# A SwiGLU feed-forward on one core: weight-block differences on GpSimd instead of VectorE

## The chip, the cores and the metric

The kernel runs on one core of one Trainium2 chip. The metric is device time of one execution in microseconds. The engines are named as in the profile: PE (TensorE matmul) and PEld (its weight load), DVE (VectorE), ACT (ScalarE), POOL (GpSimd) and SP (SyncE, here the queue that issues nearly all DMAs).

## What is computed

One encoder layer on 1024 tokens of width 1024: a token mixer, then a SwiGLU channel mixer, all in float32. The change lies in the channel mixer, with a hidden width of 2816:

```python
h = rms_norm(x) * (1 + sc2) + sh2
x = x + g2 * ((jax.nn.silu(h @ ffn_w_gate[l]) * (h @ ffn_w_up[l])) @ ffn_w_down[l])
```

## The kernel before

The hidden width is cut into NF = 22 column tiles of 128. For each tile the products with the gate and the up weights are formed as one 2x2 block product by Strassen-Winograd: seven block products instead of eight, with differences of weight blocks (T1 to T4) and of activation blocks (S1 to S4) as operands. Each float32 operand is split into a high and a low float32r part (`split`: a copy on ACT at L233, a subtraction on DVE at L239), and each block product is three passes of four 128x128 by 128x512 matmuls, so 12 matmuls (`product`, L1606).

The function `ffn` has three stages.

- **Stage one** (loop at L1655): for each tile the two products that need the plain gate weights. Their sums p1 and s1 go to DRAM (tensor `psd`).
- **Stage two** (loop at L1717): for each tile f the other five products, in the order X with T2 (PSUM tile X), Y with T1 (PSUM tile Y), X with T3, Y with block B22, X with T4. Names in the profile: `T12h`/`T12l` hold T1 and T2, `T3h`/`T3l` hold T3 and B22, `t4s` holds T4. DVE adds the partial sums between them: L1739 after the first X product, L1741 after the first Y product, L1745, L1747, L1749, then L1754 and L1756 for the second half. PE waits for L1739 before it adds T3 to X, for L1741 before it adds B22 to Y and for L1745 before it adds T4 to X. Differences of rows of the down weights and of activations, tiles x and y (both named `sx`), are formed on the way for stage three (L1743, L1751, L1759 in the first 11 tiles, L1762, L1763, L1765 in the last 11) and stored (`td`, `s3d`, `sd`, `s4d`).
- **Stage three** (L1834 on): the down projection out of the stored operands.

The weight blocks of a tile are made by `weights(f)` at L1667: loads of `wg` and `wu` (L1617, 512 KB each), two differences into `t12`, one into `wu` in place, one into `t4`, and the three splits. It is called at high priority, ahead of its tile. `wg`, `wu`, `t12` and `t4` have two buffers each, and so have the split tiles. So the load of `wu` for tile f+4 waits until the split T3l of tile f+2 has read its buffer, and the load of `wg` for tile f+4 waits until the last difference (L1678) of tile f+2 has read its. The tiles x and y share three buffers.

A scheduler writes one fixed order for each engine from the code and its priorities. Each engine, and SP's queue of DMAs too, then works strictly in that order: an instruction or a DMA that waits holds all that stand behind it.

Of the kernel before, what the change touches and what calls it, by code (L numbers as in the profile page):

```python
# [12 lines left out]
ALU = mybir.AluOpType  # L13
# [1568 lines left out]
def ffn(K, sp, S, at):  # L1582
# [4 lines left out]
    nc, d = K.nc, K.d  # L1587
    V = nc.vector
# [20 lines left out]
    def pair(t, slots, name):  # L1609

        hi, lo = (S.tile([P, NK, P], F32R, s, name + n) for s, n in zip(slots, "hl"))
        K.split(hi, lo, t)
        return [(hi[:, c], lo[:, c]) for c in (slice(0, 4), slice(4, 8))]

    def load(src, f, slot):
        t = S.tile([P, NK, P], F32, slot, src)
        nc.sync.dma_start(t, d[src][f])  # L1617
        return t
# [48 lines left out]
    def weights(f):  # L1667
        wg, wu = load("wg", f, (22, 8)), load("wu", f, (24, 9))
        t12 = S.tile([P, NK, P], F32, (26, 10), "t12")
        t4 = S.tile([P, 4, P], F32, (19, 16), "t4")  # L1670
        B11, B21, B12, B22 = wg[:, 0:4], wg[:, 4:8], wu[:, 0:4], wu[:, 4:8]
        w = {}
        V.tensor_tensor(t12[:, 0:4], B12, B11, op=ALU.subtract)
        V.tensor_tensor(t12[:, 4:8], B22, t12[:, 0:4], op=ALU.subtract)
        w["T1"], w["T2"] = pair(t12, ((28, 11), (29, 14)), "T12")
        V.tensor_tensor(B12, B22, B12, op=ALU.subtract)
        w["T3"], w["22"] = pair(wu, ((20, 12), (23, 15)), "T3")
        V.tensor_tensor(t4, B21, t12[:, 4:8], op=ALU.subtract)  # L1678
        hl = S.tile([P, 2, 4, P], F32R, (25, 13), "t4s")
        K.split(hl[:, 0], hl[:, 1], t4)  # L1680
        w["T4"] = hl[:, 0], hl[:, 1]
        return w
# [32 lines left out]
    with K.first():  # L1715
        ws = [weights(0)]
    for f in range(NF):  # L1717
        ps1 = S.tile([P, 2, H], F32, (27, 0, 1, 2), "psr")
        nc.sync.dma_start(ps1, K.psd[f])
        if f + 1 < NF:  # L1720
            with K.first():
                ws.append(weights(f + 1))
        else:
            more(3)
# [153 lines left out]
```

## Time and profile before

| | us |
|---|---|
| three runs | 1514.78, 1514.87, 1522.44 |
| median | 1514.87 |
| profiled execution, its own time | 1520.79 |
| span of the profiled execution | 1518.9 |
| PE busy | 1389.5 |
| DVE busy | 1118.4 |
| ACT busy | 542.5 |
| POOL busy | 90.9 |

The span is the time from the first to the last instruction of the profiled execution; its own time is 1.9 us longer. Busy time is summed over instructions of an engine. In the trace stage one runs from about 815 us, stage two from about 980 to 1294 us, and stage three to the end.

### The profile page before, as it was taken

To read this page: it belongs to the slowest core of one execution; us is meant where nothing else is said; L and a number is where in the kernel's file an instruction comes from. 1 tells how busy PE (TensorE), PEld (TensorE's weight loads), DVE (VectorE), ACT (ScalarE), POOL (GpSimd) and SP (SyncE) were. 2 spreads that over 40 slices of the span, in tenths; PEclk is the share of its full clock that TensorE was granted. 3 is DMA by queue.
4 is the path that set the end of the run, shared out by engine and by line. 5 is a ranking of instruction groups with operands and counts; after the bars stand their busy time and mean duration, and the time that the engine had idled before them with its cause. 6 is when DMAs were issued, how large, how long until landed. Compare 5 with 4: busy or idle time off the path is not lost.

```text
span 1518.9 us, 19510 instructions
## 1 busy us (share of the span) xinstructions
PE 1389.5 (91%) x6717; PEld 1115.8 (73%) x6717; DVE 1118.4 (74%) x2123; ACT 542.5 (36%) x973; POOL 90.9 (6%) x143
## 2 busy tenths in 40 slices
PE   2589989998998998999998999999999999999995
PEld 0366768776787767877776777887778878888884
DVE  7999977887756684687865458378777887557588
ACT  2522221232142342333545766322222222434352
POOL 2110000000101231320000000000000000000000
PEclk9789999999998999989999999999999999999998
DMA  6634366577662324476435448677776776977762
GB/s 248 196 101 146 121 198 217 181 240 222 205 195 93 114 84 154 118 250 223 151 102 180 146 164 285 230 258 249 254 246 218 234 266 239 331 236 244 238 221 110
DMA packets 160598, 300.31 MB, mean 198 GB/s; under 512 B 27871, under 2 KB 72831, under 8 KB 160500
## 3 DMA queue, kind: packets, MB, share of 16 engines
q1 hardware_dynamic: 137204, 271.77, 54.6%
q10 hardware_dynamic: 22688, 25.99, 4.8%
q0 software_dynamic: 608, 1.31, 0.3%
q8 instruction: 53, 0.87, 0.2%
q14 instruction: 45, 0.37, 0.1%
HBM read 221.12 MB, written 77.89 MB: 197 GB/s over the span
## 4 chain that ended last, share of the span: by engine, by line
PE 59%; DVE 14%; DMA 9%; issue 3%; ACT 1%; POOL 1%; SPq 0%; POOLq 0%; DVEq 0%; ACTq 0%
PE Z L1606 8%; PE X L1606 6%; PE dx L1844 6%; PE Y L1606 5%; PE gps L495 5%; PE gps L507 4%; PE dz L1844 4%; PE dy L1844 4%; PE gps L1556 3%; DMA mxw<-modw 3%; DMA wu<-wu 2%; PE nS L1429 2%; PE ops L1556 1%; PE nS L1407 1%; DVE wlo L239 1%
## 5 line engine op out<-in xcount | busy, mean ns | idle before, releaser
L495 PE MATMUL gps<-hhi,whi 128*128 128x512 f32 x320 | 130.3, 407 | 3.8 <-ACT nt L531 3.8
L495 PE MATMUL gps<-hlo,whi 128*128 128x512 f32 x320 | 128.9, 403 | 0.0
L495 PE MATMUL gps<-hhi,wlo 128*128 128x512 f32 x320 | 128.4, 401 | 0.0
L239 DVE TENSOR_TENSOR dl<-dr,dh 128x1024 fp32r<-128x1024 f32 x77 | 93.5, 1221 | 37.4 <-ACT dh L233 25.2
L233 ACT CAST dh<-dr 128x1024 fp32r<-128x1024 f32 x77 | 80.4, 1052 | 104.6 <-PE dz L1844 30.0
L1606 PE MATMUL Z<-hp,wgh 128*128 128x512 f32 x352 | 95.8, 402 | 1.0 <-ACT ps L1661 0.9
L507 PE MATMUL gps<-whi,hhi 128*128 128x256 f32 (+1 forms) x256 | 76.8, 300 | 1.5 <-ACT z L531 1.5
L1606 PEld LDWEIGHTS Z<-hp,wgh 128*128 128x128 f32 x352 | 63.6, 188 | 19.2 <-ACT ps L1661 4.7
L507 PE MATMUL gps<-whi,hlo 128*128 128x256 f32 (+1 forms) x256 | 76.8, 300 | 0.0
L507 PE MATMUL gps<-wlo,hhi 128*128 128x256 f32 (+1 forms) x256 | 76.3, 298 | 0.0
L495 PEld LDWEIGHTS gps<-hhi,whi 128*128 128x128 f32 x320 | 60.5, 189 | 19.3 <-ACT nt L531 5.0
L233 ACT CAST T3h<-wu 128x1024 fp32r<-128x1024 f32 x22 | 23.1, 1052 | 132.0 <-PE Y L1606 121.1
L495 PEld LDWEIGHTS gps<-hhi,wlo 128*128 128x128 f32 x320 | 60.2, 188 | 13.7 <-issue 1.6
L495 PEld LDWEIGHTS gps<-hlo,whi 128*128 128x128 f32 x320 | 60.4, 189 | 12.2 <-issue 0.8
L1500 DVE SCALAR_TENSOR_TENSOR mxacc<-mxw,cond,mxacc 128x512 f32<-128x512 f32 x56 | 41.9, 748 | 32.4 <-DMA mxw<-modw 32.2
L1606 PE MATMUL X<-A,t4s 128*128 128x512 f32 x264 | 63.6, 390 | 0.1
L1606 PEld LDWEIGHTS X<-A,t4s 128*128 128x128 f32 x264 | 49.5, 188 | 10.8 <-DVE uv L1745 0.5
L507 PEld LDWEIGHTS gps<-whi,hhi 128*128 128x128 f32 x256 | 49.9, 195 | 3.1 <-ACT z L531 1.9
L1606 PE MATMUL Y<-AS,T3h 128*128 128x512 f32 x176 | 45.5, 400 | 7.3 <-DVE uv L1741 7.3
L1844 PE MATMUL dx<-dh,dl 128*128 128x512 f32 x132 | 51.4, 389 | 0.0
L1844 PE MATMUL dx<-dh 128*128 128x512 f32 x132 | 51.4, 389 | 0.0
L1844 PE MATMUL dx<-dl,dh 128*128 128x512 f32 x132 | 51.4, 389 | 0.0
(521 smaller groups left out, 3511.2 us busy)
## 6 DMA issues: line engine op xcount, KB each, us to landing
wg<-wg SPq DMA_DIRECT2D x44, 512.0 KB
mxw<-modw SPq DMA_DIRECT2D x64, 256.0 KB
raw<-w_in SPq DMA_DIRECT2D x28, 512.0 KB
dr<-wd SPq DMA_DIRECT2D x55, 256.0 KB
psd<-ps SPq DMA_DIRECT2D x22, 512.0 KB
psr<-psd SPq DMA_DIRECT2D x22, 512.0 KB
wu<-wu SPq DMA_DIRECT2D x22, 512.0 KB
ad<-a SPq DMA_DIRECT2D x22, 512.0 KB
```

The source lines that it names most:

```text
L233: nc.scalar.copy(hi, src)
L239: e.tensor_tensor(lo, src, hi.bitcast(F32), op=ALU.subtract)
L495: nc.tensor.matmul(ps, lhsT=w[:, k, c], rhs=x[k][:, t], start=n == 0, stop=n == len(seq) - 1)
L507: nc.tensor.matmul(ps, lhsT=x[k][:, t], rhs=w[:, k, :N], start=n == 0, stop=n == len(seq) - 1)
L1407: nc.tensor.matmul(pb[:, :nk], lhsT=qt[r, i], rhs=ktv[r, r0:r0 + nr, f * 24:f * 24 + 40], start=True, stop=True)
L1429: nc.tensor.matmul(pb[:, 448:512], lhsT=pT[:w * 40, n], rhs=vw[:w * 40, n, c:c + 64], start=n == 0, stop=n == len(chunks) - 1)
L1500: V.scalar_tensor_tensor(acc, in0=mt, scalar=K.cond[:, k:k + 1], in1=acc, op0=ALU.mult, op1=ALU.add)
L1556: K.nc.tensor.matmul(ps, lhsT=l, rhs=r, start=n == 0, stop=n == 5)
L1606: nc.tensor.matmul(ps, lhsT=w[a][:, k], rhs=x[k][b], start=start and n == 0, stop=n == 11, skip_group_check=not start)
L1844: nc.tensor.matmul(acc[i], lhsT=a[:, 0, ts], rhs=b[:, 1], start=first and m == 0, stop=final and m == 2, skip_group_check=n in (2, 3, 5, 6))
```

## The change

The four differences of `weights` go from DVE to POOL. The splits stay where they were. One line is added, so that the lines behind it have a number higher by one in the changed kernel (L1673 becomes L1674, L1678 becomes L1679, L1743 becomes L1744).

```diff
-        V.tensor_tensor(t12[:, 0:4], B12, B11, op=ALU.subtract)
-        V.tensor_tensor(t12[:, 4:8], B22, t12[:, 0:4], op=ALU.subtract)
+        G = nc.gpsimd
+        G.tensor_tensor(t12[:, 0:4], B12, B11, op=ALU.subtract)
+        G.tensor_tensor(t12[:, 4:8], B22, t12[:, 0:4], op=ALU.subtract)
         w["T1"], w["T2"] = pair(t12, ((28, 11), (29, 14)), "T12")
-        V.tensor_tensor(B12, B22, B12, op=ALU.subtract)
+        G.tensor_tensor(B12, B22, B12, op=ALU.subtract)
         w["T3"], w["22"] = pair(wu, ((20, 12), (23, 15)), "T3")
-        V.tensor_tensor(t4, B21, t12[:, 4:8], op=ALU.subtract)
+        G.tensor_tensor(t4, B21, t12[:, 4:8], op=ALU.subtract)
```

The scheduler makes a new order out of it. On DVE, from the end of tile 5 to the start of tile 6, in the first half of stage two (numbers behind a name tell tiles apart: `uv_9384` and `a_9438` are of tile 5, `uv_9489` and x, `sx_9483`, of tile 6), before:

```order
L1747 TENSOR_TENSOR uv_9384<-Y_9383,uv_9384 128x512
L239 TENSOR_TENSOR T3l_9476<-wu_9464,T3h_9475 128x1024
L1749 TENSOR_TENSOR a_9438<-uv_9384,psr_9355 128x512
L1754 TENSOR_TENSOR psr_9355<-X_9382,psr_9355 128x512
L239 TENSOR_TENSOR t4s_9480<-t4_9467,t4s_9480 128x512
L1743 TENSOR_TENSOR sx_9483<-sx_9483 128x512
L1756 TENSOR_TENSOR a_9438<-uv_9384,psr_9355 128x512
L1739 TENSOR_TENSOR uv_9489<-X_9487,psr_9460 128x512
L1673 TENSOR_TENSOR t12_9676<-wu_9674,wg_9672 128x512
```

and in the changed kernel:

```order
L1748 TENSOR_TENSOR uv_9384<-Y_9383,uv_9384 128x512
L239 TENSOR_TENSOR T3l_9476<-wu_9464,T3h_9475 128x1024
L1750 TENSOR_TENSOR a_9438<-uv_9384,psr_9355 128x512
L1744 TENSOR_TENSOR sx_9483<-sx_9483 128x512
L1755 TENSOR_TENSOR psr_9355<-X_9382,psr_9355 128x512
L239 TENSOR_TENSOR t4s_9480<-t4_9467,t4s_9480 128x512
L1752 TENSOR_TENSOR sx_9483<-sx_9484,sx_9483 128x512
L1757 TENSOR_TENSOR a_9438<-uv_9384,psr_9355 128x512
L1740 TENSOR_TENSOR uv_9489<-X_9487,psr_9460 128x512
L1760 TENSOR_TENSOR sx_9379<-a_9438 128x512
L1742 TENSOR_TENSOR uv_9489<-Y_9488,psr_9460 128x512
L239 TENSOR_TENSOR T12l_9576<-t12_9571,T12h_9575 128x1024
```

The differences are gone from DVE, and both steps on x (`sx_9483`, L1744 and L1752) now stand ahead of L1757 of tile 5 and of L1740, the first sum of tile 6.

On SP's queue at the same place, from one load of `wu` (tile 9) to the next (tile 10), before (`td6`, `s3d5` and `ad5` are stores of tiles 6 and 5; of the two loads of `sx`, here of tile 7, the one of 128x1024 is x and the one of 128x512 is y):

```order
L1617 DMA wu_9674<-wu 128x1024
L1757 DMA ad5_135<-a_9438 128x1024
L1719 DMA psr_9775<-psd9_165 128x1024
L1760 DMA s3d5_205<-sx_9379 128x512
L1617 DMA wg_9882<-wg 128x1024
L1752 DMA td6_184<-sx_9483 128x1024
L1728 DMA sx_9588<-wd 128x1024
L1729 DMA sx_9589<-wd 128x512
L1617 DMA wu_9779<-wu 128x1024
```

and in the changed kernel, with two rows of the tile ahead:

```order
L1720 DMA psr_9670<-psd8_164 128x1024
L1729 DMA sx_9483<-wd 128x1024
L1617 DMA wu_9674<-wu 128x1024
L1753 DMA td6_184<-sx_9483 128x1024
L1758 DMA ad5_135<-a_9438 128x1024
L1617 DMA wg_9882<-wg 128x1024
L1761 DMA s3d5_205<-sx_9379 128x512
L1730 DMA sx_9589<-wd 128x512
L1720 DMA psr_9775<-psd9_165 128x1024
L1729 DMA sx_9588<-wd 128x1024
L1617 DMA wu_9779<-wu 128x1024
```

The store `s3d5` and the load of x (`sx_9588`) now stand behind the load of `wg`, and the load of x is the last before the next `wu`.

## Rows read from the trace of the kernel before

**Rows 1.** The page, part 1: busy time, share of the span and instructions of each engine.

```profile
PE 1389.5 (91%) x6717; PEld 1115.8 (73%) x6717; DVE 1118.4 (74%) x2123; ACT 542.5 (36%) x973; POOL 90.9 (6%) x143
```

**Rows 2.** Windows: both halves of stage two; stretch, its length, busy time by engine.

```profile
993.50:1139.70 146.20, 139.35 (x604) 112.42 (x603) 116.44 (x171) 33.57 (x41) 0.00 (x0) 1.00 0.73 248
1139.70:1294.20 154.50, 153.38 (x670) 124.91 (x669) 123.89 (x176) 37.27 (x45) 0.00 (x0) 1.00 0.70 240
```

**Rows 3.** Waits of PE in stage two: us in total, times, longest.

```profile
PE Y L1606 <- DVE uv L1741: 7.3, 9, 1.2
```

**Rows 4.** Timeline of PE: start, us, engine, line, operation, out and in, count.

```profile
1080.57 2.88 PE L1606 MATMUL X<-A,t4s 128*128 128x512 f32 x12
1083.29 1.30 PE L1606 MATMUL X<-AS,T12h 128*128 128x512 f32 x5
```

**Rows 5.** Timeline of SP's queue, one tile of the first half.

```profile
1067.61 1.29 SPq L1617 DMA_DIRECT2D wu<-wu  x1
...
1077.09 0.33 SPq L1617 DMA_DIRECT2D wg<-wg  x1
1078.29 0.32 SPq L1752 DMA_DIRECT2D td<-sx  x1
...
1082.40 0.33 SPq L1729 DMA_DIRECT2D sx<-wd  x1
1082.83 0.38 SPq L1617 DMA_DIRECT2D wu<-wu  x1
```

**Rows 6.** Timeline of DVE, first half of stage two; in brackets the idle time ahead.

```profile
1065.71 0.69 DVE L1747 TENSOR_TENSOR uv<-Y,uv 128x512 f32<-128x512 f32 x1 [1.91 <-PE Y L1606]
1066.32 1.22 DVE L239 TENSOR_TENSOR T3l<-wu,T3h 128x1024 fp32r<-128x1024 f32 x1
...
1072.83 0.69 DVE L1673 TENSOR_TENSOR t<-wu,wg 128x512 f32<-128x512 f32 x1 [1.20 <-DMA wu<-wu]
...
1077.59 0.68 DVE L1751 TENSOR_TENSOR sx<-sx 128x512 f32<-128x512 f32 x1
...
1087.07 0.69 DVE L1673 TENSOR_TENSOR t<-wu,wg 128x512 f32<-128x512 f32 x1 [0.38 <-DMA wu<-wu]
...
1139.69 0.69 DVE L1747 TENSOR_TENSOR uv<-Y,uv 128x512 f32<-128x512 f32 x1 [1.91 <-PE Y L1606]
```

**Rows 7.** Waits of SP's queue in stage two: us in total, times, longest.

```profile
SPq L1617 <- DVE t L1678: 35.4, 17, 4.3
```

**Rows 8.** Groups of POOL: count, then busy us, mean ns, then idle time before.

```profile
L239 POOL TENSOR_TENSOR hlo<-tm,hhi 128x512 fp32r<-128x512 f32 x8 | 11.9, 1492 | 47.3 <-DVE hhi L235 47.3
...
L429 POOL TENSOR_TENSOR acc<-acc,pr 128x512 f32<-128x512 f32 x7 | 10.1, 1449 | 13.6 <-ACT pr L427 13.3
L1349 POOL TENSOR_TENSOR mhh<-mtt,mnd 128x512 f32<-128x512 f32 x8 | 9.2, 1152 | 44.8 <-DVE mnd L1347 44.8
```

**Rows 9.** Timeline of POOL, at two places where DVE works too.

```profile
13.08 3.10 POOL L429 TENSOR_TENSOR acc<-acc,pr 128x512 f32<-128x512 f32 x2 [0.23 <-ACT pr L427]
...
675.45 1.04 POOL L1349 TENSOR_TENSOR mhh<-mtt,mnd 128x512 f32<-128x512 f32 x1 [7.49 <-DVE mnd L1347]
```

**Rows 10.** Timeline of DVE at the same two places (su, sn, acc, mw: SBUF; mS: PSUM).

```profile
10.36 0.69 DVE L688 SCALAR_TENSOR_TENSOR su<-sn,su 128x512 f32<-128x512 f32 x1
...
13.32 1.75 DVE L424 SCALAR_TENSOR_TENSOR acc<-mw,cond,acc 128x512 f32<-128x512 f32 x1
...
675.41 0.75 DVE L1328 TENSOR_TENSOR msd<-msd,mS 128x256 f32<-128x256 f32 x2
```

**Rows 11.** Timeline of SP's queue, second half: 256 KB stores and the loads that wait for them.

```profile
1163.79 0.32 SPq L1766 DMA_DIRECT2D s4d<-sx  x1
1167.02 0.32 SPq L1731 DMA_DIRECT2D sx<-s3d  x1
...
1207.59 0.32 SPq L1766 DMA_DIRECT2D s4d<-sx  x1
1213.24 0.32 SPq L1731 DMA_DIRECT2D sx<-s3d  x1
```

## The prediction

> **What bounds the kernel now.** I read the page first: PE is busy for 1389.5 us, DVE for 1118.4, POOL for 90.9 [rows 1]. The change lies in stage two, so I cut stage two into windows. In the first 146.2 us, from the sum L1747 of tile 0 to that of tile 10, PE is busy for 139.35 us and idle for 6.85; in the last 154.5 us it is idle for only 1.12 [rows 2]. The waits of PE name the sum L1741 on DVE for 7.3 us [rows 3]. More than these 8 us can't be won in stage two.
>
> PE's own pace: 12 matmuls take 2.71 us from start to start [rows 4], so the five products of a tile take 13.6 us. But from 1065.71 to 1139.69 five tiles pass, 14.8 us each [rows 6]. DVE isn't full there. The 14.8 us come from a loop through SP's queue [rows 5, 6]: a load of wu is issued at 1067.61 and L1673 starts on it at 1072.83 (5.2 us); the differences run up to 1077.09, when the load of wg that waits for L1678 goes out (4.3); the store td follows at 1078.29, behind L1751 (1.2); the load of y waits for it until 1082.40 (4.1); the next load of wu goes at 1082.83 (0.4). The sum is 15.2 us. The reader should see that SP waits in order: for L1678 alone the queue stood still for 35.4 us in 17 waits [rows 7]. All that stands behind the load of wg depends on how soon the differences are done.
>
> **What the change removes.** 88 differences leave DVE, 4 per tile. Starts of neighbours on DVE lie 0.6 us apart [rows 6], so DVE has 2.4 us more per tile of at least 13.6. That pays only where DVE makes PE wait, which is the 8 us above.
>
> **What it adds.** POOL has nothing to do in stage two [rows 2], so four differences of any likely length fit into a tile. What counts is how late the last of them ends. The price of one is bounded by POOL's own 128x512 operations: 1.04 us at the least [rows 9], 1.45 and 1.49 in the mean for those with two full operands [rows 8]. These means hold waiting: in 13.08 to 16.18 two of them took 3.10 us while a DVE operation with SBUF operands only took 1.75 instead of 0.69 [rows 9, 10]. Each evidently waits for the other's whole instruction: 1.04 for POOL and 0.6 for DVE make up most of either length. With an operand in PSUM it is not so: two at 675.41 took 0.75 together beside a POOL operation of 1.04. I take 1.04 per difference, plus 0.6 for each DVE operation between two SBUF tiles that gets in between, and 1.04 on that DVE operation when it must wait.
>
> The same rows are weighed against a rule. The Trainium skill, "GPSIMD Engine Reference", section 4.1 "Engine selection", says that two-input elementwise work belongs on VectorE, since GpSimd takes about twice as long; section 3.1 gives 4497 ns for 2048 elements, of which 512 would be 1.1 us, an estimate. By it four differences would take 4.5 us where I use 4.2, and the end would come about 1.5 us later.
>
> **What it moves.** In two tiles of three in the first half, the changed order has SP issue the load of wg, then the store s3d, the load of y, the load of psr, the load of x (which waits for that store, since x and y share three buffers) and the next load of wu. In the third, s3d stands ahead of wg, and y waits for the store td. On DVE, the steps on x (L1744 and L1752) stand ahead of L1757 and of L1740, for which PE waits. So in the first kind a loop over two tiles closes, which I add up from a load of wu on:
>
> - The load lands after 4.7 us, the mean of 5.2 and 4.2 [rows 5, 6].
> - Four differences on POOL, with three DVE operations in between: 4 x 1.04 + 3 x 0.6 = 6.0. Without any collision it is 4.2.
> - The issue of wg: 0.4, as between neighbours [rows 5].
> - The store s3d until the load of x can go: 256 KB stores of the second half took 3.2 and 5.7 [rows 11], the 512 KB td of this half 4.1 [rows 5]. I take 3.6, between the shortest and td.
> - The load of x, 512 KB: 4.2, the faster load of wu.
> - DVE from L1744 to the end of L1740: six operations of 0.6, and two of them wait for POOL, which has just begun the next tile's differences: 3.6 + 2 x 1.04 = 5.7.
> - PE: X with T3 and Y with B22, 5.4 [rows 4].
> - L1748 and the split T3l, 0.6 + 1.2 = 1.8 [rows 6], then the load of wu two tiles on is issued.
>
> That is 31.8 us for two tiles, 15.9 for one. The third kind goes by SP's queue alone: 4.7 + 6.0 + 0.4 + 4.1 + 0.4 = 15.6. The mean is 15.8, 2.2 over PE's pace. For nine tiles PE idles 19.8 us where it now idles 6.85: **13 us more**.
>
> In the second half there are no steps on x of this kind; only the loads of wu can come late. SP's loop there: 4.7 + 6.0 + 0.4 + 4.4 (the mean of the two stores) + 0.8 for two loads of sx = 16.3, 2.7 over the pace, for seven loads, 19 us in all. Against that stands a lead. A load of wu goes out 1.8 us after Y with B22 of its tile less four, and its T12 split can't begin before Y with T1 of its tile less two, 2.7 + 13.6 + 5.4 = 21.8 us after the same point. That leaves 20.0, of which landing and two differences need about 8: 12 us in hand. I take 19 less 12 or a little less: **6 us**; at the lowest it is 0.
>
> Stage three holds no differences, and stage one only those of the first tiles, ahead of their use: I cost both at nothing. If that cover were gone, stage two would start later by four differences, 4.2 us. What waits on POOL's own queue is differences alone. The sum is +19 us: the profiled execution would go from 1520.8 to 1539.8. That execution was 5.9 us over the median of the three runs, so against the median 1514.87 I forecast **1534 us**. A measurement of this kernel tells 0.5%, 7.6 us, from no change.
>
> **Rivals.**
>
> 1. POOL's work hides wholly, and PE's waits go. Without collisions, with the short store and the fast load, the loop is 4.2 + 4.2 + 0.4 + 3.2 + 4.2 + 3.6 + 5.4 + 1.8 = 27.0 for two tiles, under 27.2: PE would run through. The 6.85 us go and the time is 1508. For it speaks that DVE is idle for some 20% of stage two [rows 2]; against it, that x and wu land nearly together, so that POOL runs just when DVE has its SBUF operations. It decides as soon as 4.6 us of the loop's 31.8 fall away. Chance 0.12.
> 2. Relief and waits cancel: about half of the collisions, 14 to 15 us per tile, 1512 to 1522. Chance 0.13.
> 3. A difference costs what the dear rows say, 1.49, beside collisions. Then the four take 7.8, L1740 comes 0.9 later, and with stores of 4.1 and loads of 5.2 the loop is 36.5, 18.2 per tile: 9 x 4.6 less 6.85 is +35, and the lead of the second half is used up, for up to 33 more. The time is 1545 to 1583. For it: all means but one [rows 8]. Against it: the collisions of those rows are counted twice. Chance 0.20.
> 4. That the change doesn't do what it says is excluded: the order has all 88 differences on POOL.
>
> **How the numbers follow.** The forecast, 15 to 17 us per tile in the first half and 0 to 12 us in the second, has 0.55 and a range of its own from 1523 to 1545. Faster by over 0.5% (under 1507.3) is only the outer edge of rival 1, since 8 us of waits are all there is: 0.04. Within 0.5%: the rest of rival 1 and rival 2, 0.21. Slower: forecast and rival 3, 0.75. The range 1511 to 1558 leaves out most of rival 1 and the upper half of rival 3, some 0.2.
>
> **What would show it.** Right: POOL near 90.9 + 100 to 140 us, its differences at 1.04 alone and 1.6 to 2.2 beside DVE; DVE operations in stage two of 1.2 to 1.75 where they were 0.69; SP waiting for POOL ahead of the loads of wg, for more than the 35.4 us; DVE idle ahead of L1744 for the load of x; PE idle ahead of X with T3 for L1740, some 25 us in stage two; tiles of unequal length in a pattern of three. Wrong: tiles of 13.6 us throughout, or POOL's differences that touch no DVE operation. If POOL is slow but PE still waits for L1742 or for T12l, my loop is the wrong one.

## The result and the profile after

| | before | after |
|---|---|---|
| median of 6 runs each, us | 1517.15 (1514.78 to 1522.44) | 1573.39 (1567.95 to 1575.97) |
| profiled execution, us | 1520.79 | 1574.4 |

The ratio is 1.0358, 95% interval 1.0334 to 1.0381: slower by 56 us. The sign is that of the forecast, the size is three times as large; the time lies above the range, in the region of rival 3. All times given below are medians of fast runs; a single slow one, of e9 (1593.1 us), is left out.

The busy line of the page after, to be read against [rows 1]:

```profile
PE 1406.3 (89%) x6717; PEld 1128.2 (72%) x6717; DVE 1109.8 (71%) x2035; ACT 542.2 (34%) x973; POOL 228.3 (15%) x231
```

POOL gained 137.4 us. DVE lost 88 instructions, 60 us at 0.68 each, but only 8.6 us of busy time. PE is busy 16.8 us longer with the same matmuls.

The windows of stage two after, cut at the sums L1748 of tiles 0, 10 and 21 (stretch, length, busy time of PE, PEld, DVE, ACT and POOL, granted clock, DMA share, GB/s):

```profile
996.20:1171.30 175.10, 145.66 (x587) 116.55 (x586) 113.19 (x130) 32.17 (x40) 64.52 (x40) 0.91 0.57 204
1171.30:1345.30 174.00, 158.78 (x663) 128.88 (x662) 123.72 (x142) 37.35 (x45) 50.13 (x32) 0.95 0.63 215
```

Between the same sums (L1747 there) in the kernel before, both halves in one stretch:

```profile
993.50:1291.60 298.10, 290.13 (x1262) 235.16 (x1261) 237.95 (x344) 70.70 (x85) 0.00 (x0) 1.00 0.71 243
```

Its halves are 146.2 and 151.9 us long. So stage two is 51.0 us longer, 29 in the first half and 22 in the second. PE's idle time there went from 8.0 to 44.7 us, which is 36.7 of the 51; the other 14.3 are PE's own busy time, at a granted clock of 0.91 and 0.95 where [rows 2] had 1.00. DVE's busy time in both windows is 236.9 us with 272 instructions; before it was 237.9 with 344. The relief of DVE has vanished.

What PE and SP's queue wait for after (us in total, times, longest), PE from 800 to 1400 us, SP from 980 to 1400:

```profile
PE X L1606 <- DVE uv L1740: 44.0, 13, 7.9
PE Z L1606 <- ACT ps L1661: 4.0, 1, 4.0
```

```profile
SPq L1617 <- POOL t L1679: 106.3, 17, 11.7
SPq L1696 <- POOL t L1679: 22.6, 2, 11.5
```

PE no longer waits for the sum of the first Y product [rows 3] but for that of the first X product, ahead of X with T3. SP stands still for POOL's last difference three times as long as it did for DVE's [rows 7]. The groups of POOL say what a difference costs in the mean:

```profile
L1679 POOL TENSOR_TENSOR t<-wg,t 128x512 f32<-128x512 f32 x22 | 37.2, 1691 | 5.8 <-PE Z L1606 5.8
...
L1674 POOL TENSOR_TENSOR t<-wu,wg 128x512 f32<-128x512 f32 x22 | 31.3, 1423 | 482.8 <-DMA wu<-wu 257.6 <-DVE sx L1744 57.5 <-DVE T3l L239 34.6
```

The four timelines that follow show one turn of the loop of the first half (from 1069 us) and one of the second (from 1223 us). SP's queue after:

```profile
1069.64 0.39 SPq L1617 DMA_DIRECT2D wu<-wu  x1
...
1081.65 0.33 SPq L1617 DMA_DIRECT2D wg<-wg  x1
1082.03 0.42 SPq L1761 DMA_DIRECT2D s3d<-sx  x1
1082.51 0.42 SPq L1730 DMA_DIRECT2D sx<-wd  x1
1083.03 0.43 SPq L1720 DMA_DIRECT2D psr<-psd  x1
1088.13 0.33 SPq L1729 DMA_DIRECT2D sx<-wd  x1
...
1107.63 0.33 SPq L1617 DMA_DIRECT2D wu<-wu  x1
...
1223.98 1.00 SPq L1617 DMA_DIRECT2D wu<-wu  x1
...
1236.59 0.33 SPq L1617 DMA_DIRECT2D wg<-wg  x1
...
1241.21 0.32 SPq L1732 DMA_DIRECT2D sx<-s3d  x1
...
1242.10 0.38 SPq L1617 DMA_DIRECT2D wu<-wu  x1
```

POOL after:

```profile
1075.18 1.27 POOL L1674 TENSOR_TENSOR t<-wu,wg 128x512 f32<-128x512 f32 x1 [11.77 <-DVE sx L1752]
1076.53 1.61 POOL L1675 TENSOR_TENSOR t<-wu,t 128x512 f32<-128x512 f32 x1
1078.10 2.27 POOL L1677 TENSOR_TENSOR wu<-wu 128x512 f32<-128x512 f32 x1
1080.33 1.29 POOL L1679 TENSOR_TENSOR t<-wg,t 128x512 f32<-128x512 f32 x1
...
1230.19 1.30 POOL L1674 TENSOR_TENSOR t<-wu,wg 128x512 f32<-128x512 f32 x1 [11.68 <-DVE a L1750]
...
1234.85 1.72 POOL L1679 TENSOR_TENSOR t<-wg,t 128x512 f32<-128x512 f32 x1
```

DVE after:

```profile
1091.58 0.69 DVE L1744 TENSOR_TENSOR sx<-sx 128x512 f32<-128x512 f32 x1 [6.05 <-DMA sx<-wd]
...
1093.38 1.76 DVE L1752 TENSOR_TENSOR sx<-sx 128x512 f32<-128x512 f32 x1
1095.06 1.75 DVE L1757 TENSOR_TENSOR a<-uv,psr 128x512 f32<-128x512 f32 x1
1096.73 0.68 DVE L1740 TENSOR_TENSOR uv<-X,psr 128x512 f32<-128x512 f32 x1
...
1105.78 0.69 DVE L1748 TENSOR_TENSOR uv<-Y,uv 128x512 f32<-128x512 f32 x1 [2.05 <-PE Y L1606]
1106.38 1.22 DVE L239 TENSOR_TENSOR T3l<-wu,T3h 128x1024 fp32r<-128x1024 f32 x1
...
1231.96 1.77 DVE L1757 TENSOR_TENSOR a<-uv,psr 128x512 f32<-128x512 f32 x1
1233.77 1.67 DVE L1763 TENSOR_TENSOR sx<-a,sx 128x512 f32<-128x512 f32 x1
1235.36 1.75 DVE L1764 TENSOR_TENSOR sx<-sx,a 128x512 f32<-128x512 f32 x1
1237.04 0.68 DVE L1766 TENSOR_TENSOR sx<-a,sx 128x512 f32<-128x512 f32 x1
1237.64 0.68 DVE L1740 TENSOR_TENSOR uv<-X,psr 128x512 f32<-128x512 f32 x1
```

PE after:

```profile
1090.15 1.07 PE L1606 MATMUL Y<-AS,T12l 128*128 128x512 f32 x4
1097.56 3.75 PE L1606 MATMUL X<-AS,T3h 128*128 128x512 f32 x8 [6.33 <-DVE uv L1740]
...
1238.46 2.99 PE L1606 MATMUL X<-AS,T3h 128*128 128x512 f32 x8 [2.84 <-DVE uv L1740]
```

The reader should see the chain that the forecast described. SP issues wu at 1069.64; POOL works from 1075.18 to 1081.62; only then wg goes, and behind it s3d, y, psr and, once s3d has landed, x at 1088.13. DVE sits idle ahead of L1744 for 6.05 us until that load lands, two of the operations behind it meet POOL, and L1740 ends at 1097.41. PE has idled 6.33 us, and its next eight matmuls take 3.75 us instead of 1.98, at a granted clock of 0.50, which is 1.2 GHz:

```profile
1097.56:1101.30 3.74, 3.74 (x9) 2.96 (x10) 3.14 (x3) 0.00 (x0) 2.06 (x2) 0.50 0.53 170
```

In the second half neither PE nor DVE waits for a load. There the differences, which start at 1230.19, fall on L1757, L1763 and L1764, each 1.67 to 1.77 instead of 0.68, and L1740 behind them is late by 2.84.

The Trainium skill, "SBUF — State Buffer", section "SBUF: two separate sides", states the rule for this: VectorE and GpSimd share a port pair that one instruction holds to its end, and VectorE needs it when both inputs lie in SBUF. These rows agree: L1757 and L1752 with two SBUF inputs took 1.75, L1740 with one in PSUM 0.68.

### The profile page after: what moved, and what is told of

The parts are those of the page before. It is cut to its first block, busy times and chain, and to the rows that moved or that the text cites. A ratio compares the mean times of both kernels' runs of the same rounds, so it can differ in the third digit from the quotient of the medians.

```text
span 1572.6 us, 19581 instructions
## 1 busy us (share of the span) xinstructions
PE 1406.3 (89%) x6717; PEld 1128.2 (72%) x6717; DVE 1109.8 (71%) x2035; ACT 542.2 (34%) x973; POOL 228.3 (15%) x231
## 5 line engine op out<-in xcount | busy, mean ns | idle before, releaser
L1674 POOL TENSOR_TENSOR t<-wu,wg 128x512 f32<-128x512 f32 x22 | 31.3, 1423 | 482.8 <-DMA wu<-wu 257.6
L1606 PE MATMUL X<-AS,T3h 128*128 128x512 f32 x176 | 57.4, 480 | 44.5 <-DVE uv L1740 44.0
L1606 PEld LDWEIGHTS X<-AS,T3h 128*128 128x128 f32 x176 | 39.5, 233 | 58.9 <-issue 49.0
L1606 PEld LDWEIGHTS Z<-hp,wgh 128*128 128x128 f32 x352 | 64.7, 191 | 22.7 <-ACT ps L1661 7.7
```

What stands on the lines that cost most here:

```text
L1606: nc.tensor.matmul(ps, lhsT=w[a][:, k], rhs=x[k][b], start=start and n == 0, stop=n == 11, skip_group_check=not start)
L1674: G.tensor_tensor(t12[:, 0:4], B12, B11, op=ALU.subtract)
```

## The experiments

Two theories stood against each other. **Queue**: SP's in-order queue waits, ahead of a load of wg, for POOL's last difference, and that closes a loop longer than PE's 13.6 us. **Collisions**: POOL's instructions and DVE's stretch each other, and DVE becomes late by that alone. A third came up on the way and is taken up in e12 to e14, **order**: DVE is late because the steps on x stand ahead of L1740.

**e1, T4's difference ahead of T3's.**

```diff
+        G.tensor_tensor(t4, B21, t12[:, 4:8], op=ALU.subtract)
         G.tensor_tensor(B12, B22, B12, op=ALU.subtract)
-        G.tensor_tensor(t4, B21, t12[:, 4:8], op=ALU.subtract)
```

> The changed kernel with one thing exchanged on POOL alone: the difference for T4 (into t4, the last reader of wg) is made third and the one for T3 fourth. The orders of PE, DVE, ACT and SP stay as they are. Theory of the queue (SP's load of wg waits for the last difference, and x, y and psr stand behind it): wg goes out one difference, about 1.7 us, sooner; the loop over two tiles of the first half shrinks by as much, some 0.8 us per tile, 6 to 9 us in all, and a little in the second half: 1562 to 1568 us. Theory of collisions (POOL's instructions and DVE's stretch each other, and that alone makes DVE late): the same instructions run at nearly the same places, so 1573 within 4 us.

Measured: 1571.93, ratio 1.0367 (1.0340 to 1.0394). It tells nothing of either theory. The scheduler still put T3's difference third, which doesn't need the result of T2, so every engine had the changed kernel's order and the run is a second sample of it.

**e2, collisions on top of the kernel before.**

```diff
+        for _ in range(4):
+            nc.gpsimd.tensor_tensor(t44[:, 1], t12[:, 0:4], t12[:, 4:8], op=ALU.subtract)
```

> The kernel before, differences on DVE, plus four POOL operations per tile of the same shape (128x512, SBUF to SBUF) that read t12 and write a spare half of t4's buffer; nobody waits for their result, and the orders of PE, DVE, ACT and SP are those of before. Theory of collisions: DVE's operations between SBUF tiles go from 0.69 to 1.75 us where POOL runs; four to six of them a tile are 4 to 6 us of DVE work in a tile of 13.6, so 15 to 45 us more, 1530 to 1560. Theory of the queue: no load waits for POOL, so 1515 to 1523, at most the few differences on DVE that come late.

Measured: 1567.22, ratio 1.0345 (1.0312 to 1.0378), more than either theory said. Stage two took 344.9 us, DVE was busy for 284 us of it where it had been 238. And SP was held longer too, by DVE's last difference (L1681 here), which now met POOL:

```profile
SPq L1617 <- DVE t L1681: 62.7, 17, 5.0
```

In [rows 7] this was 35.4. So collisions can cost as much as the whole change, but they do it at least partly through the same queue, and this run doesn't part the two; e2 with its loads on another queue wasn't run.

**e3 and e4, loads of wg and wu from POOL's queue**, in the changed kernel and in the kernel before.

```diff
-        wg, wu = load("wg", f, (22, 8)), load("wu", f, (24, 9))
+        wg, wu = load("wg", f, (22, 8), nc.gpsimd), load("wu", f, (24, 9), nc.gpsimd)
```

> The changed kernel with the loads of wg and wu of stage two issued from POOL's own queue instead of SP's, so that the stores and the loads of x, y and psr no longer stand behind a load that waits for POOL. The DVE order changes a little (the steps on x move). Theory of the queue: the load of x comes in time, L1744 no longer holds L1740, and the first ten tiles take about 140 to 150 us instead of 175: some 25 to 35 us less, 1538 to 1550. Theory of collisions: the differences still run beside DVE's operations, so most of the loss stays: 1560 or more.

> The kernel before (differences on DVE) with the same loads issued from POOL's queue. It tells what the queue costs without any POOL arithmetic. Theory of the queue: the loop of 14.8 us per tile in the first ten tiles goes down to the 13.6 us of PE, up to 7 us less: 1507 to 1512. If the loads are issued more dearly from POOL, or if DVE's order gets worse, no gain: 1515 to 1525.

Measured: e3 1523.18, ratio 1.0032 (1.0010 to 1.0055), its first ten tiles 138.9 us; e4 1531.51, ratio 1.0107 (1.0076 to 1.0138). The time of e3 is 15 us under what even the queue theory said, which had counted on the first half alone. With SP free, 50 of the 56 us go although all differences stay on POOL. Stage two takes 292.2 us in e3, 5.9 less than before, but begins 6.3 later. e4 missed both expectations: it is slower by 1.1%, 6.5 us over the second one. PE waits there for the same two sums of DVE, L1741 (9.4 us) and L1739 (6.0); why wasn't followed up.

**e5, only wg from POOL's queue.** The orders of PE, DVE and ACT are those of e3.

> As e3, but only the loads of wg go out from POOL's queue; those of wu stay on SP. The orders of PE, DVE and ACT are those of e3. SP then never waits for POOL, but a load of wu still stands behind the loads of x that wait for stores. If the hold of SP by POOL is what costs (and nothing else), the time is that of e3, 1520 to 1528. If what counts is the moment at which wu lands, and so whether POOL's four differences fall on DVE's chain L1757, L1763, L1764, L1766 ahead of L1740 (as in the changed kernel's second half) or behind it (as in e3), then SP's loads of x still set that moment and part of the loss comes back: 1530 to 1550.

Measured: 1522.76, ratio 1.0034 (1.0011 to 1.0057), the time of the first alternative. The place of the collisions shows all the same: the first ten tiles took 134.9 us, the rest 160.6 where e3 had 153.2. One tile of the second half, DVE and PE of e5:

```profile
1210.90 1.78 DVE L1764 TENSOR_TENSOR sx<-sx,a 128x512 f32<-128x512 f32 x1
1212.61 1.78 DVE L1766 TENSOR_TENSOR sx<-a,sx 128x512 f32<-128x512 f32 x1
```

```profile
1215.13 2.09 PE L1606 MATMUL X<-AS,T3h 128*128 128x512 f32 x8 [1.55 <-DVE uv L1740]
```

and of e3:

```profile
1214.88 1.78 DVE L1766 TENSOR_TENSOR sx<-a,sx 128x512 f32<-128x512 f32 x1
```

```profile
1217.41 2.09 PE L1606 MATMUL X<-AS,T3h 128*128 128x512 f32 x8 [0.45 <-DVE uv L1740]
```

One stretched operation ahead of L1740 costs PE 0.45 us of idle time (tiles of 14.3), two cost 1.55 (15.4), three in the changed kernel 2.84 and a lower clock (18.4). How many are hit goes with the moment at which the first difference starts: 1.7 us behind the start of t4s on DVE in e5, 2.4 in e3, and 0.7 ahead of it in the changed kernel.

**e6, the last step of the second half (L1766) behind the next tile's L1740.**

> The changed kernel with the last step on x of a tile of the second half (L1766, for s4d) written behind the sums L1740 and L1742 of the next tile; in DVE's order it then stands behind L1740 instead of ahead of it, SP's order is unchanged. If the second half is slow because DVE's SBUF operations ahead of L1740 are stretched by POOL, each of seven or eight slow tiles loses one operation of 0.6 to 1.75 us ahead of L1740: its excess of some 4 us falls by 0.6 to 2, the second half (174 us) by 6 to 14, and the time is 1559 to 1567. If the second half is slow because wu or x come late through SP's queue, a later s4d makes it no faster: 1572 or more.

Measured: 1569.11, ratio 1.0332 (1.0288 to 1.0376); the intervals of this and of the change overlap, and the time lies between the two alternatives. In the trace the second half took 170.9 us instead of 173.9. Four of its tiles became short (14.5, 15.9, 14.7, 15.1), the three behind them long (18.0, 19.7, 18.4), with DVE waiting for the load of s3d and for a buffer that sd still held. What fewer collisions freed, SP's loop of some 18 us took back.

**e7 and e10, mixed.** e7 is e3 for tiles 4 to 21, with the code of before for tiles 0 to 3; e10 is the same with the differences of all tiles on DVE.

```diff
-        G = nc.gpsimd
+        G = nc.gpsimd if f >= 4 else V
```

> e3 for tiles 4 to 21, and for the tiles 0 to 3, whose weights are made while stage one still runs, the code of before (differences on DVE, loads on SP). e3 entered stage two 6.3 us later than before and then took 5.9 us less for it. If the late start comes from the first tiles' differences on POOL and their loads, this one keeps the gain alone: 1510 to 1514, under the kernel before. If the late start comes from elsewhere, 1518 to 1524.

> e7 with the differences of all tiles on DVE: the loads of wg and wu of tiles 4 to 21 from POOL's queue, no arithmetic there. It tells whose gain e7's is. If it is the queue's alone: 1505 to 1511, as e7. If POOL's differences are needed for it (e4 against e3 says so: 1531 and 1523), 1514 to 1526.

Measured: e7 1507.86, ratio 0.9931 (0.9907 to 0.9954); e10 1527.28, ratio 1.0059 (1.0037 to 1.0082). e7 beats the kernel before, by 2 us more than was said, and e10, a little over the second alternative, shows that it needs the differences on POOL: the same edit as the change, for 18 of the 22 tiles and on a kernel whose SP queue doesn't wait for it, gains about 19 us. The late start came from the first tiles, as expected, though e7 doesn't part their differences from their loads. In the changed kernel ACT waited for POOL's second difference of tile 0 while stage one still ran, and PE for ACT (the 4.0 us above; in the kernel before, PE's wait for L1661 is 0.9). ACT and PE in the changed kernel:

```profile
934.41 1.05 ACT L233 CAST T12h<-t 128x1024 fp32r<-128x1024 f32 x1 [4.66 <-POOL t L1675]
```

```profile
939.53 3.43 PE L1606 MATMUL Z<-hp,wgh 128*128 128x512 f32 x8 [3.98 <-ACT ps L1661]
```

**e8, T3 alone on POOL.**

> Only the difference for T3 on POOL, the other three on DVE: wg waits for DVE alone, one POOL operation of 1.28 us per tile. If the loss goes with the hold of SP by POOL, none is left: 1513 to 1522, and DVE is relieved by 0.6 us a tile. If it goes with collisions, one of four remains, some 10 to 15 us: 1525 to 1535.

Measured: 1522.56, ratio 1.0031 (1.0007 to 1.0055), half a microsecond over what the queue theory allowed. SP no longer waits for POOL; for DVE's last difference it waits 30.9 us, about as in [rows 7].

**e9, a third buffer for wg.**

```diff
-        wg, wu = load("wg", f, (22, 8)), load("wu", f, (24, 9))
+        wg, wu = load("wg", f, (22, 8, 16)), load("wu", f, (24, 9))
```

> The changed kernel with a third buffer for wg (room is made by letting both t4 tiles share one). All differences stay on POOL, all loads on SP. The orders of PE and POOL are those of the changed kernel, that of DVE but for a handful of rows, so x's steps still stand ahead of L1740; only the reason for which SP waits ahead of a load of wg is gone, since its buffer is free long before. If it is SP's hold by POOL's last difference that costs, SP's 106 us of waits for POOL go, x and wu come in time and the time is 1518 to 1535, with POOL still meeting DVE. If the four differences on POOL cost by themselves (length and collisions), at least half of the 56 us stays: 1545 to 1573.

Measured: 1574.01, ratio 1.0357 (1.0310 to 1.0404). The edit didn't do what it was to do: the scheduler used the buffer to issue each load of wg a tile earlier, and it waited for the then latest difference as before, 52.8 us in the first half and 59.0 in the second. So it tells nothing of the two theories.

**e11, e7 with the step of e6.**

> e7 with the last step on x of the second half (for s4d) behind the next tile's L1740, as in e6. In e7 PE still idles some 0.45 us in each of six tiles of the second half, because one DVE operation ahead of L1740 meets POOL; this should go: 1504 to 1507 where e7 had 1508. If the later s4d holds the loads of x instead, 1508 to 1515.

Measured: 1505.62, ratio 0.9908 (0.9877 to 0.9939), as said, and the lowest median of this study; its interval overlaps that of e7. Its stage two, between the same sums, in windows:

```profile
991.30:1276.90 285.60, 285.60 (x1262) 236.49 (x1261) 213.80 (x272) 70.82 (x85) 132.08 (x106) 1.00 0.73 254
```

PE is busy for all of the 285.6 us, 21 tiles of 13.6, and DVE now has the relief: 213.8 us.

**e12, x's steps behind L1740.** L1744 gets the sum u as an operand that it doesn't use.

```diff
-            V.tensor_tensor(x[:, 0], x[:, 1], x[:, 0], op=ALU.subtract)
+            V.scalar_tensor_tensor(x[:, 0], in0=x[:, 1], scalar=u[:, 0:1], in1=x[:, 0], op0=ALU.bypass, op1=ALU.subtract)
```

> The changed kernel in which the first step on x (L1744) also names the sum u of its own tile as an operand that it doesn't use, so that it and L1752 can only stand behind L1740 on DVE. Differences on POOL, loads on SP; SP's load of wg still waits for POOL's last difference. (e9 left that wait in place: the loads of wg merely moved one tile further ahead, and SP waited for POOL 111.8 us as against 106.3, so it told nothing of the hold.) If the first half is slow because x comes late through the held queue and its steps stand ahead of L1740, PE no longer waits for x: the first ten tiles go from 175 to 138 to 150 us, the second half stays at 174, and the time is 1537 to 1552. If the first half is slow through late differences or collisions alone, it stays over 165 and the time over 1562.

Measured: 1574.15, ratio 1.0367 (1.0334 to 1.0400): nothing gained, and the first ten tiles still took 172.5 us, as the second alternative said. So the place of x's steps ahead of L1740 isn't what costs; PE's wait moved to the next sum. In the tile shown no DVE operation lengthens a difference on POOL, and SP waited for POOL all the same. PE's waits in stage two, and POOL, in e12:

```profile
PE Y L1606 <- DVE uv L1742: 24.8, 9, 4.9
PE X L1606 <- DVE uv L1740: 17.9, 8, 3.2
```

```profile
1090.07 1.27 POOL L1674 TENSOR_TENSOR t<-wu,wg 128x512 f32<-128x512 f32 x1 [11.88 <-DVE T12l L239]
1091.42 1.29 POOL L1675 TENSOR_TENSOR t<-wu,t 128x512 f32<-128x512 f32 x1
1092.66 1.28 POOL L1677 TENSOR_TENSOR wu<-wu 128x512 f32<-128x512 f32 x1
1093.89 1.30 POOL L1679 TENSOR_TENSOR t<-wg,t 128x512 f32<-128x512 f32 x1
```

The loads of wu before and after these went out at 1084.48 and 1101.53: a loop of 17.05 us with POOL's part at 5.1: 5.6 us until the first difference, 5.1 for the four, 0.4 for wg, 5.5 from the store td (1095.65) until y can go (1101.11), 0.4. So in this tile SP's queue alone, without collisions on POOL, is 3.4 us over PE's pace.

**e13 and e14, one order, with and without the hold.** Both place x's steps behind L1746, where e3 and e5 had them; e14 also issues wg from POOL's queue. PE, DVE and ACT have the same orders in both.

> The changed kernel with both steps on x placed behind L1746 on DVE, where e3 and e5 have them (L1744 is moved there in the code and names v as an unused operand); loads of wg on SP as in the changed kernel, so that SP waits for POOL's last difference. PE, DVE and ACT have the same orders as in e14. Theory of the queue: SP's loop through POOL (load of wu, four differences, load of wg, a store's landing, next load of wu) sets the tile, whatever DVE does: the first ten tiles take 160 us or more, the time is 1555 or more. Theory of the order (e3 and e5 were fast because x's steps moved): the first ten tiles take 135 to 145 us and the time is 1535 to 1545, since the second half stays slow.

> e13 with one thing changed: the loads of wg go out from POOL's queue, so that SP doesn't wait for POOL. The orders of PE, DVE and ACT are those of e13, and POOL's differences run on the same engine. Theory of the queue: the first ten tiles take 134 to 142 us, the second half 153 to 162, the time is 1518 to 1530. Theory of the order: no difference to e13 in the first half. Theory of collisions: both over 1555.

Measured: e13 1566.35, ratio 1.0314 (1.0292 to 1.0336); e14 1519.01, ratio 1.0002 (0.9985 to 1.0020). The windows of the first ten tiles of e13 and of e14:

```profile
994.20:1155.40 161.20, 144.57 (x616) 116.94 (x616) 113.48 (x130) 33.51 (x42) 62.07 (x39) 0.98 0.65 226
```

```profile
990.00:1126.40 136.40, 136.40 (x603) 112.96 (x602) 116.70 (x131) 33.65 (x40) 69.44 (x49) 1.00 0.79 269
```

The pair differs in the queue of one load, and the times by 47 us. Both times and the windows came out as the queue theory said. In these ten tiles DVE is stretched as much in e14 (116.7 us) as in e13 (113.5), and PE never idles (the profiled run of e14 is its fastest, 7 us under the median). That settles it for 47 of the 56 us: SP's wait for POOL's last difference is what the change costs. What collisions cost without that wait shows in the second half of e14, where PE idles 5.6 us, in tiles of 14.3 and 15.4; in the changed kernel it idles 15.2 there.

## Why the prediction was wrong

**In the first half the mechanism was the right one.** POOL gained 137 us (100 to 140 said), differences beside DVE took 1.6 to 2.3 us, DVE's operations up to 1.78, SP's waits for POOL went to 129 us, DVE idled ahead of L1744 for the load of x, PE ahead of X with T3 (44.0 us, 25 said), and the tiles of the first half came in threes (24.3, 14.1, 17.8; 22.7, 15.2, 13.6; 22.6, 14.1, 13.6 us).

**Where the missing time lies.** The profiled executions differ by 53.6 us where 19 were forecast. PE's idle time grew by 22.6 us in the first half (13 said) and by 14.1 in the second (6 said). PE's own busy time in stage two grew by 14.3, a term that the forecast put at nothing, and stage two began 2.7 later.

**The step that failed is PE's pace, taken from a PE that never idles: 5.4 of the 31.8 us of the two-tile loop, and nothing in the sum.** The turn shown above, from the load of wu at 1069.64 to that at 1107.63, took 38.0:

| term | forecast | measured | from to |
|---|---|---|---|
| load of wu to first difference | 4.7 | 5.5 | 1069.64 to 1075.18 |
| four differences | 6.0 | 6.4 | 1075.18 to 1081.62 |
| wg, then s3d | 0.4 | 0.4 | 1081.62 to 1082.03 |
| s3d until x goes | 3.6 | 6.1 | 1082.03 to 1088.13 |
| x to L1744 | 4.2 | 3.5 | 1088.13 to 1091.58 |
| L1744 to the end of L1740 | 5.7 | 5.8 | 1091.58 to 1097.41 |
| X with T3, Y with B22 | 5.4 | 8.4 | 1097.41 to 1105.78 |
| L1748, T3l, next wu | 1.8 | 1.9 | 1105.78 to 1107.63 |

Two terms carry 5.5 of the 6.2, but only one of them does so each time. In the two other turns that end in a long stall of PE (39.2 and 35.9 us) PE's term is again 8.4 and 8.2. Of PE's ten idle times from 2.4 to 7.9 us in stage two, nine are followed by eight matmuls of 2.5 to 3.75 us instead of 1.98 (not the one of 2.54); behind the shorter ones, up to 1.5 us, they take 2.1. So a stall lengthens the loop in which it stands.

**The transfers were the second term.** The store s3d held x for 4.1 to 4.2 us in the five other turns of this kind, though wg, s3d, y and psr go out just as close together there; why it took 6.1 here is open. Store and load of x together took 10.5, 9.5 and 8.5 us in the three turns with a long stall, where 7.8 was said. SP's queue alone was put at 15.6; the turn of e12, in which no difference is lengthened, took 17.05, with td holding y for 5.5 us where 4.1 was said and the first difference 5.6 behind the load of wu where 4.7 was said.

**The price of a difference** was too low at 1.04, the cheapest row [rows 9]; alone it takes 1.27 to 1.30. Four of them are 5.1 instead of 4.2 before any collision. The Trainium skill, "GPSIMD Engine Reference", section 3.1 gave an estimate of 1.1 us, which this trace doesn't bear out either. With collisions the four took 6.5 in the mean of the first ten tiles, nearer to the forecast's 6.0 than to rival 3's 7.8. That rival 3's time, 1545 to 1583, holds the result is in part luck: neither PE's slower term nor the second half as it came stands in it.

**The second half** was forecast at 6 us, from wu coming late for PE after a lead of 12 us. Here the mechanism was wrong, not only the size. The loop of SP was there, 18.1 us (1223.98 to 1242.10) where 16.3 was said; most of the difference is the load of wu, 6.2 instead of 4.7. But PE waited for L1740, not for the splits: in each slow tile the differences fall on the chain L1757, L1763, L1764, L1766. I had counted collisions in POOL's time and on x's chain, not there. The lead was not what decided.

**The cover of stage one**, costed at nothing, was gone too: stage two began 2.7 us later, behind ACT's wait for POOL.

**Rival 1** failed at its condition: of the terms that it shortened to bring the loop to 27.0 (load, differences, store, DVE's part), none came as short in this turn. What it said of hidden work holds in part once SP's queue is out of the loop: the first ten tiles of e14 show collisions without harm, e11 DVE's relief too.

## What to carry to other kernels

When work moves to a slower engine, look up who else waits for its last read: here a DMA load in an in-order queue, and behind it all the stores and loads that had nothing to do with it. Add up that loop with transfers as long as they are when the queue lets several go at once (in e12 td held y for 5.5 us where the forecast took 4.1), and with PE at the clock that it has after an idle time. The same edit was worth 3.6% more time with the loads in SP's queue and 0.3% more with them in the queue of the engine that frees their buffers (e3). Mixed with the old code for the first tiles it took 0.7% less (e7), and 0.9% less with L1766 moved as well (e11).

## What the runs showed of the hardware that I had not expected

- A float32 difference of 128x512 on POOL takes 1.27 to 1.30 us alone, against 0.68 on DVE, and up to 2.37 beside DVE; a DVE operation that meets it takes up to 1.78.
- Moving 72 of 344 instructions of stage two off DVE lowered its busy time from 237.9 to 236.9 us only: what it no longer computes it spends waiting for POOL. The Trainium skill, "Perfetto Trace Analysis", section "Optimizing Scalar/DVE Operations", warns that moving work between these two might not help, since they share a port; here the trace agrees. In e11, where it is mostly the split T12l that meets a difference (up to 2.3 us instead of 1.22), the relief is there: 213.8 us.
- PE's granted clock in stage two, of which 1.00 is 2.4 GHz, fell to 0.91 and 0.95 in the mean of the two halves, behind idle times of 2.4 to 7.9 us; PE's busy time there grew by 14.3 us, in e13 by 10.7 (300.8 against 290.1).
- Loads of 512 KB issued from POOL's own queue mostly cost POOL 0.53 to 0.57 us each and did not come later for it: in e3 a difference starts 3.6 us after the issue of its wu (1196.63 to 1200.24), where the changed kernel's turn shown above has 5.5.
